# Seven block products for eight in the output phase of a hybrid decoder step

## The chip, the cores and the metric

The kernel runs on one core of one Trainium2 chip. The metric is device time in microseconds (us) of one execution. TensorE (PE) multiplies; VectorE (DVE), ScalarE (ACT) and GpSimd (POOL) work on tiles in SBUF, and DVE and ACT also on PE's accumulators in PSUM; SyncE (SP) issues the DMAs. Each engine runs its own instructions in order and waits on semaphores for the others.

## The reference

One layer of a decoder on 2048 prompt tokens and 32 sample tokens (8 sequences of 4), width 1024, everything float32:

```
h = rmsnorm(x);  p = h @ w_in                    # conv, rwkv and gate columns
y_c = bg * conv(cg * xin) * silu(zc)             # short convolution branch
y_r = (groupnorm(rwkv7_scan(...)) + bonus) * silu(zr)
m   = sigmoid(gc) * (y_c @ w_out_c) + sigmoid(gr) * (y_r @ w_out_r)
out = rmsnorm(x + m @ w_o, final_g)              # plus the new states
```

`w_out_c`, `w_out_r` and `w_o` are 1024 x 1024 each. The change concerns the last two lines of it.

## The kernel before

**Precision.** A float32 operand is kept as two float32r tiles, a rounded high part and the low rest. A product is three matmuls per 128 rows of the contraction: high weight by high data, low by high, high by low. The parts of a weight are made once (ACT copies the high part, DVE subtracts the low one), stored to DRAM (`keep`) and loaded again as 1 MB tiles `whl` for later sets. Four `whl` buffers exist; `take_w` hands out the next tile of the fixed list `order` and starts the loads of the following three.

**Sets.** The prompt is cut in four sets of 512 tokens (numbers 0 to 3 in the code, one to four in this text); the fourth carries the 32 sample tokens as well (544 columns). The first part of the program, four stretches of some 600 us, projects each set with 81 blocks of `w_in` (24 matmuls of 512 columns per block of 128 output channels, accumulator `ip`) and interleaves the scan of the rwkv branch, pair of heads by pair of heads. Its small matmuls and its DVE and ACT work are generators (`Side`) that a planner, the class `Clock`, spreads over the stretch with weights (`SIDES`) and costs of its own; on DVE and ACT the planned order is then fixed. The branch results y_c and y_r and the gates go to DRAM (`yc`, `yr`, `gc`, `gr`).

**Output phase.** Each set has three stages of 1024 x 1024: c (`w_out_c`), r (`w_out_r`) and out (`w_o`). Stages c and r give m transposed, eight blocks of 128 channels each (`proj`, tiles `ip`); DVE multiplies by 1 + tanh gate, adds c and r and splits m into `MH` and `ML` (`merged`). Stage out takes 128 tokens of m as the stationary operand and 512 columns of `w_o` as the moving one (accumulator `po`): per set two halves of four kp steps of 24 matmuls. Then x is added (`xo`), the squares are summed by ACT, and `finish` scales the row and stores it; the reciprocal root is a power on GpSimd (`rsq`). The order is: c of sets one and two at the end of the first part (`merge_first`, over the last scan), then r and out of set two, r and out of set one, then c, r and out of set three and of set four. Set four's 544 columns run as 256 and 288. `load_y` brings y and splits it for the next set while out runs. Each of the three weights is split the first time it is used, which lies in this phase.

In the profile nearly every compute row carries the line of a helper (L264), and every DMA row L337 or L264; rows are told apart by their tiles.

Of the kernel before, what the change touches and what calls it, by code (L numbers as in the profile page):

```python
# [16 lines left out]
P = 128  # L17
# [7 lines left out]
SIDES = {"first": 8.0, "late": 14.0, "keys": 30.0, "solve": 30.0, "merge": 8.0, "close": 12.0, "load": 8.0, "samp": 20.0, "out": 12.0, "prep": 10.0, "y": 4.0, "chain": 45.0, "zero": 1.0}  # L25
# [319 lines left out]
def hybrid_kernel(tc, x_prompt, x_sample, state_conv, state_shift, state_rwkv, norm_g, w_in, conv_w,  # L345
# [26 lines left out]
    wraw_p = Raws(ctx.enter_context(tc.tile_pool(name="wraw", bufs=1)), NB * P, 4, clock)  # L372
    whl_p = clock.pooled(ctx.enter_context(tc.tile_pool(name="whl", bufs=4)), "whl", 4)
    dram = ctx.enter_context(tc.tile_pool(name="dram", bufs=1, space=DRAM))
    ps_ip = clock.pooled(ctx.enter_context(tc.tile_pool(name="ps_ip", bufs=3, space=PSUM)), "ps_ip", 3)

    yc_d = [[dram.tile([P, 2, NTT[t]], F32, name=f"yc{t}_{b}") for b in range(NB // 2)] for t in range(NSETS)]
    yr_d = [[dram.tile([P, 2, NTT[t]], F32, name=f"yr{t}_{b}") for b in range(NB // 2)] for t in range(NSETS)]
    gc_d = [[dram.tile([P, NTT[t]], F32, name=f"gc{t}_{b}") for b in range(NB)] for t in range(NSETS)]
    gr_d = [[dram.tile([P, NTT[t]], F32, name=f"gr{t}_{b}") for b in range(NB)] for t in range(NSETS)]  # L380
# [9 lines left out]
    def w_advance(dma, split, load):  # L390
        while state["dma"] < min(dma, len(order)):
            _, src, _, there = order[state["dma"]]
            if not there:
                raw = wraw_p.tile()
                SP.dma_start(out=raw.rearrange("p (kt n) -> p kt n", n=src.shape[1]),
                             in_=src.rearrange("(kt p) n -> p kt n", p=P))
                raws[state["dma"]] = raw
            state["dma"] += 1
        while state["split"] < len(order):
            i = state["split"]  # L400
            _, src, keep, there = order[i]
# [3 lines left out]
            if there:  # L405
                SP.dma_start(out=hl.bitcast(F32), in_=keep)
# [4 lines left out]
            parts_[i] = tuple(hl[:, k].rearrange("p (kt n) -> p kt n", n=src.shape[1]) for k in range(2))  # L411
# [167 lines left out]
    nwt = clock.pooled(ctx.enter_context(tc.tile_pool(name="nwt", bufs=1)), "nwt", 1)  # L579
# [111 lines left out]
    r0 = 0  # L691
# [182 lines left out]
    def conv_blocks(th, b):  # L874
# [61 lines left out]
        def bg_end():  # L936
            SP.dma_start(out=yc_d[th][b // 2][:, b % 2, :], in_=o["cv"][:, 0:nt])
            o.clear()

        def gate(nm, base, dst):  # L940
# [10 lines left out]
            def end():  # L951
                SP.dma_start(out=dst[th][b], in_=g["t"][:, 0:nt])
                tmp.free(g["t"])
# [486 lines left out]
    def rwkv_out(th, p, o):  # L1440
# [40 lines left out]
        SP.dma_start(out=yr_d[th][p // 2][:, p % 2, :], in_=yo[:, 0:nt])  # L1481
# [15 lines left out]
    def merge_first(th, b):  # L1497
# [4 lines left out]
        def fetch():  # L1502
            o, t, bb = gates.pop(0)
            o["g"] = tmp.tile([P, TW], F32, name="tmp")
            SP.dma_start(out=o["g"][:, 0:NT], in_=gc_d[t][bb])
# [11 lines left out]
        def end():  # L1517
            SP.store(gc_d[th][b], o["g"][:, 0:NT], lambda g=o["g"]: tmp.free(g))
# [4 lines left out]
    def load_first(nm, th, hf):  # L1523
# [7 lines left out]
        for q in range(NB // KG):  # L1531
            raws.append(ring[len(turn) % len(ring)])
            turn.append(q)
            for i in range(KG // 2):
                SP.dma_start(out=raws[q][:, 2 * i:2 * i + 2, :],
                             in_=(yc_d if nm == "c" else yr_d)[th][q * KG // 2 + i][:, :, cs])
# [4 lines left out]

    EDGE = 3
    plan = []
# [3 lines left out]
    for th in range(NSETS):  # L1547
        for p in range(NB):
# [18 lines left out]
    def keep(key, src):  # L1567
        if key not in seen:
            seen.add(key)
            kind = (key[0],) + key[2:]  # L1570
# [3 lines left out]
            order.append((key, src, scratch[kind], there))  # L1574
# [3 lines left out]
    MERGE = [("c", 0)] + [x for b in range(NB) for x in ([("c", b + 1)] if b + 1 < NB else []) + [("r", b)]]  # L1578
    OUTW = [(half, kp) for half in range(2) for kp in range(NB // 2)]
    ORDER3 = list(PRE[::-1]) + [th for th in range(NSETS) if th not in PRE]  # L1580
    for th in ORDER3:
        for nm, b in [x for x in MERGE if x[0] == "r" or th not in PRE]:
            wsrc = w_out_c if nm == "c" else w_out_r
            keep(("o" + nm, th, b), wsrc[0][:, b * P:(b + 1) * P])
        for half, kp in OUTW:
            keep(("o", th, half, kp), w_o[0][kp * 2 * P:(kp + 1) * 2 * P, half * 512:(half + 1) * 512])

    def main_stream(parts):
        for x, c0, c1 in parts:
            kind = (x.key[0], x.key[1]) if x.key[0] in ("oc", "or") else ("prep", x.key[1])  # L1590
# [3 lines left out]
    def load_y(th, nm):  # L1594

        src = yc_d if nm == "c" else yr_d
        nt = NTT[th]
        h, l = (XH, XL) if nm == "c" else (RH, RL)

        def load(b, j):  # L1600
            raw = o2.tile([P, 1024], F32, name="yraw")[:, 0:nt]
            SP.dma_start(out=raw, in_=src[th][b][:, j, :])
            return raw
        raws = [load(0, 0)]
        for b in range(NB):
            if b + 1 < NB:
                raws.append(load((b + 1) // 2, (b + 1) % 2))
            raw = raws.pop(0)
            A.copy(h[:, b, 0:nt], raw)
            V.tensor_tensor(out=l[:, b, 0:nt], in0=raw, in1=h[:, b, 0:nt].bitcast(F32), op=ALU.subtract)  # L1610
            yield 1
# [84 lines left out]
    for th, hv, p, nx in plan:  # L1696
        total = length(hv)
# [4 lines left out]
        else:  # L1702
# [3 lines left out]
            before = (th, p)  # L1706
            if (th, p) == (0, 0):
                Side(late_setup(), "late").over(0, 0.9 * total)
        e = EDGE / 2 * NB
        if end_(th, p):  # L1710
            run_pair(th, p, total, True)
            f = [nx] + [nx + NB * NB * (i + 1) for i in range(len(PRE))]
            behind, start = job["out", LAST * NB + p - 1], nx - 6 * NB
            for (nm, t), at, back in zip([("c", t) for t in PRE] + [("r", FIRST)], f, [EDGE * NB * (NTT[th] - HN) / NT] + [e] * len(PRE)):
                for hf, x in enumerate((at - back, at)):
                    behind = job["o" + nm, t, hf] = Side(load_first(nm, t, hf), "prep", [behind], gate=x + 0.01).over(start, x)
# [5 lines left out]
    finish_sides()  # L1722
    clock.planning = False
# [12 lines left out]
    ps_o = ph3.enter_context(tc.tile_pool(name="ps_o", bufs=5, space=PSUM))  # L1736
    fg = o1.tile([P, D], F32, name="fg")
    nc.gpsimd.dma_start(out=fg, in_=final_g.partition_broadcast(P))
    WM = NT + NSAMP
    RH, RL, MH, ML = (o1.tile([P, NB, WM], F32R, name=nm) for nm in ("RH", "RL", "MH", "ML"))  # L1740

    def merged(th, b, g, gc, c0, c1, ps):

        V.scalar_tensor_tensor(out=g[:, c0:c1], in0=g[:, c0:c1], scalar=1.0, in1=ps[:, 0:c1 - c0], op0=ALU.add, op1=ALU.mult)
        V.tensor_tensor(out=g[:, c0:c1], in0=gc[:, c0:c1], in1=g[:, c0:c1], op=ALU.add)
        A.activation(out=MH[:, b, c0:c1], in_=g[:, c0:c1], func=AF.Identity, scale=0.5)
        V.scalar_tensor_tensor(out=ML[:, b, c0:c1], in0=g[:, c0:c1], scalar=0.5, in1=MH[:, b, c0:c1].bitcast(F32),
                               op0=ALU.mult, op1=ALU.subtract)

    def merge_second(b):  # L1750

        o = {}

        def fetch():
            for nm, src in (("r", gr_d), ("c", gc_d)):
                o[nm] = o2.tile([P, WM], F32, name="gt", bufs=6)
                SP.dma_start(out=o[nm][:, 0:NT], in_=src[FIRST][b])

        def begin():
# [125 lines left out]
```

## Time and profile before

| | us |
|---|---|
| median of three runs (lowest, highest) | 3168.12 (3167.94, 3169.0) |
| span of the profiled execution | 3166.9 |
| PE busy in it | 3071.6 (97%) |
| DVE busy | 1972.5 (62%) |
| ACT busy | 1256.6 (40%) |
| GpSimd busy | 316.2 (10%) |
| stretch from the end of c to the last matmul (2690 to 3154) | 464, of it PE busy 458.8 |
| from the last matmul to the end | 12.9 |

The profiled execution is 1.2 us shorter than the median of the runs. A span is counted from the first to the last instruction. Busy times of an engine are shares over the whole program, while the stages differ: in the first part DVE is busy 64 to 78% of the time, in the output phase 37%. Matmuls overlap in the pipeline, so the price of one is the distance between starts, not its duration.

### The profile page before, as it was taken

The page shows a single profiled execution, that of the slowest core. Times are in us where ns is not written, and L with a number is a line of the kernel's source. Part 1 is how long each engine was busy: PE and PEld are TensorE (multiplying, and loading weights), DVE is VectorE, ACT ScalarE, POOL GpSimd, SP SyncE. Part 2 cuts the span into 40 slices and gives each one's busy share as a digit, 9 for nine tenths or more (in the row PEclk, how much of TensorE's full clock was granted, in tenths as well). Part 3 has the DMA queues.
Part 4 walks back from the last instruction along what each step waited for, and adds up shares of the span by engine and source line. Part 5 has one row for each costly group of instructions (what it writes and reads, how often), then busy time and mean ns, then how long its engine had stood idle before and what let it go on. Part 6 is the DMA issues. An engine that isn't in the chain of part 4 may idle for free. (4 is left out here: it accounts for less than half of the span.)

```text
span 3166.9 us, 55564 instructions
## 1 busy us (share of the span) xinstructions
PE 3071.6 (97%) x21530; PEld 2630.7 (83%) x21530; DVE 1972.5 (62%) x5444; ACT 1256.6 (40%) x2583; POOL 316.2 (10%) x521
## 2 busy tenths in 40 slices
PE   7899999999999999999999999999999998999998
PEld 6678777888888888787888889998999988878896
DVE  5577777766666666666656676777677753443432
ACT  4455555544343444444444444444444431211201
POOL 2011111111111111111111110000000010000000
PEclk9899999999999999999999999999999999999999
DMA  8677777754444444444444444443444469988863
GB/s 269 234 241 234 227 226 227 239 192 162 151 164 166 166 163 162 163 163 151 161 164 164 159 152 138 149 141 131 147 148 136 165 226 313 346 324 316 315 240 120
DMA packets 252253, 621.89 MB, mean 196 GB/s; under 512 B 35210, under 2 KB 153091, under 8 KB 198230
## 3 DMA queue, kind: packets, MB, share of 16 engines
q1 hardware_dynamic: 251846, 617.82, 56.9%
q8 instruction: 170, 2.79, 0.3%
q14 instruction: 93, 0.76, 0.1%
q0 software_dynamic: 144, 0.52, 0.0%
HBM read 457.34 MB, written 160.94 MB: 195 GB/s over the span
## 5 line engine op out<-in xcount | busy, mean ns | idle before, releaser
L264 PE MATMUL ip<-XH,whl 128*128 128x512 f32 (+3 forms) x7776 | 2112.6, 352 | 34.3 <-DVE tmp L264 11.0
L264 PEld LDWEIGHTS ip<-XH,whl 128*128 128x128 f32 x7776 | 1346.6, 191 | 190.2 <-DVE whl L264 12.2
L264 PE MATMUL ip<-XL,whl 128*128 128x512 f32 (+3 forms) x3888 | 1364.7, 351 | 0.1
L264 PEld LDWEIGHTS ip<-XL,whl 128*128 128x128 f32 x3888 | 741.5, 191 | 74.5 <-issue 5.6
L264 DVE TENSOR_TENSOR tt<-Mi,X 128x60 f32<-128x60 f32 (+24 forms) x992 | 215.3, 217 | 29.9
L264 DVE TENSOR_TENSOR X<-X,tt 128x60 f32<-128x60 f32 (+24 forms) x992 | 211.7, 213 | 32.3
L264 DVE SCALAR_TENSOR_TENSOR S<-pb,pe,sp 64x64 f32<-64x64 f32 x512 | 143.6, 280 | 135.7 <-PE pb L264 128.3
L264 ACT ACTIVATE tmp<-ip,vec 128x512 f32<-128x512 f32 (+2 forms) x174 | 102.6, 592 | 281.0 <-PE ip L264 276.7
L264 ACT ACTIVATE sp<-S,pe 128x128 f32<-128x128 f32 x256 | 102.8, 402 | 265.0 <-DVE S L264 264.1
L264 ACT COPY SV<-pb 64x128 f32<-64x128 f32 x256 | 66.0, 258 | 325.0 <-PE pb L264 323.0
L264 PE MATMUL po<-whl,MH 128*128 128x512 f32 x544 | 170.4, 394 | 0.0
L264 DVE TENSOR_TENSOR UB<-pa,P 64x64 f32<-64x64 f32 x512 | 109.9, 215 | 95.8 <-PE pa L264 78.9
L264 DVE TENSOR_TENSOR whl<-wraw,whl 128x1024 fp32r<-128x1024 f32 x105 | 132.8, 1267 | 50.5 <-ACT whl L264 42.1
L264 ACT CAST whl<-wraw 128x1024 fp32r<-128x1024 f32 x105 | 108.9, 1040 | 58.9 <-PE ip L264 36.9
L264 PE MATMUL ip<-RH,whl 128*128 128x512 f32 (+2 forms) x512 | 128.4, 342 | 2.1 <-DMA whl<-w_or 1.9
L264 PEld LDWEIGHTS po<-whl,MH 128*128 128x128 f32 x544 | 102.3, 188 | 23.6
L264 ACT COPY Xbd<-Mi 32x256 f32<-32x256 f32 x128 | 88.2, 689 | 72.0 <-DVE Mi L264 69.8
L264 DVE SCALAR_TENSOR_TENSOR gt<-gt,ip 128x288 f32<-128x288 f32 (+2 forms) x67 | 36.5, 544 | 125.4 <-PE ip L264 100.8
L264 ACT ACTIVATE tmp<-ip 128x512 f32<-128x512 f32 (+2 forms) x126 | 63.0, 500 | 124.3 <-PE ip L264 124.0
L264 PEld LDWEIGHTS pb<-UB,Xbd 128*128 128x128 f32 x512 | 86.7, 189 | 30.5 <-PE ip L264 9.2
L264 PEld LDWEIGHTS pa<-S,AR 128*128 128x128 f32 x512 | 89.9, 190 | 26.5 <-DVE S L264 12.1
L264 DVE TENSOR_TENSOR GM<-pt,mask_p 128x512 f32<-128x512 f32 x128 | 82.6, 686 | 45.8 <-PE pt L264 45.6
(495 smaller groups left out, 3914.4 us busy)
## 6 DMA issues: line engine op xcount, KB each, us to landing
wraw<-in_w_in_dram SPq DMA_DIRECT2D x81, 512.0 KB
whl<-w_k SPq DMA_DIRECT2D x24, 1024.0 KB
whl<-w_r SPq DMA_DIRECT2D x24, 1024.0 KB
whl<-w_v SPq DMA_DIRECT2D x24, 1024.0 KB
whl<-w_z SPq DMA_DIRECT2D x24, 1024.0 KB
whl<-w_xin SPq DMA_DIRECT2D x24, 1024.0 KB
whl<-w_cg SPq DMA_DIRECT2D x24, 1024.0 KB
whl<-w_zc SPq DMA_DIRECT2D x24, 1024.0 KB
```

The source lines that it names most:

```text
L264: r = f(*a, **k)
```

## The change

**Arithmetic.** Two sets are taken as one product. Write a weight as 2 x 2 blocks of 512 x 512 and the data of two sets as 2 x 2 blocks too (half of the channels by set). Instead of eight block products, seven are made (Winograd's form), on sums and differences of blocks. This is done in five stages: r and out of sets one and two (pair 0), then c, r and out of sets three and four (pair 1). Stage c of sets one and two keeps its eight blocks of 128 channels per set, but stands elsewhere: set one and the first three blocks of set two at the end of the first part, the other five at the start of the output phase.

**Weights.** The sums of weight blocks (four per weight; of `w_r` block 21 alone is not needed) are made by `comb`, a new side that starts with set two and is spread over sets two and three (weight 276). It loads 128 x 512 pieces `q`, splits each piece or sum into `qs` (ACT copy, DVE subtraction) and stores it to DRAM `units`. In the output phase all weights are loaded ready from there; no weight is split in it.

**Data.** `make(n, j)` builds the operand of product n: sums of blocks (DVE, in stage out partly GpSimd), then ACT's high part and DVE's low part, into one of three rooms: `UA`, and the former `XH` and `XL`. It runs two products ahead. A merge product is 4 groups j of 12 matmuls; its accumulators stay in PSUM across products, so that shared partial sums are added by PE; `merge_out` copies (ACT) or adds, multiplies by the gate (DVE), and for stage r adds into M, on GpSimd except for the last product. `out_done` adds an output product to x. For pair 1 the 2 x 528 columns run as 264 and 264 with the same weights. The 32 sample rows of out are 32 matmuls of 64 stationary columns (`US`).

**Layout.** `yc`, `yr`, `gc` and `gr` are stored by pairs of sets; set four's stores are three DMAs instead of one (`put`).

```diff
-SIDES = {"first": 8.0, "late": 14.0, "keys": 30.0, "solve": 30.0, "merge": 8.0, "close": 12.0, "load": 8.0, "samp": 20.0, "out": 12.0, "prep": 10.0, "y": 4.0, "chain": 45.0, "zero": 1.0}
+SIDES = {"first": 8.0, "late": 14.0, "keys": 30.0, "solve": 30.0, "merge": 8.0, "close": 12.0, "load": 8.0, "samp": 20.0, "out": 12.0, "prep": 10.0, "y": 4.0, "chain": 45.0, "zero": 1.0, "comb": 276.0}
+    def put(dst, th, src):
+        c = th % 2 * HW[th // 2]
+        SP.dma_start(out=dst[:, c:c + NT], in_=src[:, 0:NT])
+        if th == LAST:
+            for i in range(2):
+                c = i * HW[1] + NT
+                SP.dma_start(out=dst[:, c:c + NSAMP // 2], in_=src[:, NT + i * (NSAMP // 2):NT + (i + 1) * (NSAMP // 2)])
+    def part_of(w, key, j, src, scale=1.0):
+        hl = qs[turns[0] % 2]
+        turns[0] += 1
+        yield 1, [src]
+        A.activation(out=hl[:, 0], in_=src, func=AF.Copy, scale=scale)
+        yield 1, [hl[:, 0]]
+        V.scalar_tensor_tensor(out=hl[:, 1], in0=src, scalar=scale, in1=hl[:, 0].bitcast(F32), op0=ALU.mult, op1=ALU.subtract)
+        SP.store(units[w][key][j // 2][:, :, j % 2 * 4 * P:(j % 2 + 1) * 4 * P], hl.bitcast(F32))
+    def combined(dst, a, b, op):
+        V.tensor_tensor(out=qr[dst], in0=qr[a], in1=qr[b], op=op)
+    def comb():
+        for w, src in (("c", w_out_c[0]), ("r", w_out_r[0]), ("o", w_o[0])):
+            for j in range(4):
...
+                    for q in ("11", "12", "21", "22") if w == "c" else ("11", "12", "22"):
+                        yield from part_of(w, q, j, qr[q])
+                    combined("22", "21", "22", add)
+                    yield from part_of(w, "s1", j, qr["22"])
...
-                for t in PRE:
-                    cm = [merge_first(t, b) for b in range(NB)]
-                    hv += by_halves(cm[:EDGE]) + whole(cm[EDGE:-EDGE]) + by_halves(cm[-EDGE:])
+                cm = [merge_first(0, b) for b in range(NB)]
+                hv += by_halves(cm[:EDGE]) + whole(cm[EDGE:-EDGE]) + by_halves(cm[-EDGE:])
+                hv += by_halves([merge_first(1, b) for b in range(EDGE)])
+    STAGES = [("r", 0), ("o", 0), ("c", 1), ("r", 1), ("o", 1)]
+    PRODUCTS = {"m": ("11", "s2", "s3", "22", "12", "s1", "s4"), "o": ("21", "11", "t2", "t3", "t4", "t1", "22")}
+            if (th, p) == (1, 0):
+                job["comb"] = Side(comb(), "comb").over(0, sum(length(x[1]) for x in plan if x[0] in (1, 2) and x[2] is not None))
-    ps_o = ph3.enter_context(tc.tile_pool(name="ps_o", bufs=5, space=PSUM))
+    acc = [ps_o.tile([P, 2, 512], F32, name=f"acc{j}") for j in range(NP)]
+    ROOMS = [o1.tile([P, 2 * NP * WQ], F32R, name="UA")] + [t.rearrange("p a b -> p (a b)")[:, 0:2 * NP * WQ] for t in (XH, XL)]
+    def make(n, j, parts=(0, 1)):
...
+        if w != "o":
+            t = at({0: "11", 2: "12", 3: "12", 4: "21", 5: "11", 6: "22"}.get(k, "11"))
+            if k == 1:
+                op(at("11"), at("12"), at("11"), sub, V)
+                t = o2.tile([P, WQ], F32, name="st")[:, 0:wd]
+                op(t, at("22"), at("11"), sub, V)
...
+        else:
+            t = at({0: "y1", 1: "x1", 3: "x1", 4: "y2", 5: "x2", 6: "y1"}.get(k, "x1"))
+            if k == 2:
+                op(at("x1"), at("x1"), at("x2"), sub, V)
+                t = Y["21"][:, j, 0:wd]
+                op(t, at("y2"), at("x1"), sub, V)
+            if k == 5:
+                op(t, t, at("y2"), add, G)
+            if k == 6:
+                op(t, t, at("y2"), sub, G)
+                op(t, t, at("x1"), add, G)
+        A.copy(room[:, 0, j, 0:wd], t)
+        V.tensor_tensor(out=room[:, 1, j, 0:wd], in0=t, in1=room[:, 0, j, 0:wd].bitcast(F32), op=sub)
+    def merge_out(w, d, k, j):
...
+        if k < 3:
+            A.copy(dst, ps)
+            return
+        g = gate_for(w, d, q, j)
+        if k == 3:
+            gate_mul(dst, ps, view(g))
+        else:
+            V.tensor_tensor(out=dst, in0=dst, in1=ps, op=ALU.add)
+            gate_mul(dst, dst, view(g))
+        if w == "r":
+            (V if q == "x2" else G).tensor_tensor(out=M[q][:, j, 0:HW[d]], in0=M[q][:, j, 0:HW[d]], in1=R[q][:, j, 0:HW[d]], op=ALU.add)
+    def merge_phase(n):
+        for j in range(NP):
+            hook(n, j)
+            if j % 2 == 0:
+                wt = take_w((w, d, PRODUCTS["m"][k], j // 2))
+            for kt in range(NP):
+                wh, wl = (x[:, j % 2 * NP + kt, :] for x in wt)
+                for i, (w_, m) in enumerate(((wh, 0), (wl, 0), (wh, 1))):
+                    for a in range(1 + d):
...
+            merge_out(w, d, k, j)
+            make(n + 2, j)
+    def out_done(d, k, j):
+        V.tensor_tensor(out=o, in0=o, in1=acc[j][:, 0, :], op=ALU.add)
+        if k in (1, 4, 5, 6):
+            square(o, r, half)
+            if k > 4:
+                finish(r, [(o_at(d, x, j), x_rows(d, x, j, y_prompt)) for x in (q[0] + "1", q[0] + "2")])
```

Three places where the order moves. The first is PE where the output phase handles its last two sets. Rows before, at the end of r of set four:

```order
L264 MATMUL ip<-RH,whl 128x288 x2
L264 MATMUL ip<-RL,whl 128x288
L264 MATMUL ip<-RH,whl 128x288 x2
L264 MATMUL ip<-RL,whl 128x288
L264 MATMUL po<-whl,MH 128x512 x2
L264 MATMUL po<-whl,ML 128x512
```

and with the change, the step from out of pair 0 to c of pair 1 (`XL`, `UA` are rooms):

```order
L264 MATMUL acc_29709<-whl,XH 128x512 x6
L264 MATMUL acc_29710<-whl,XH 128x512 x6
L264 MATMUL acc_29707<-XL,whl 128x264 x24
L264 MATMUL acc_29708<-XL,whl 128x264 x24
L264 MATMUL acc_29709<-XL,whl 128x264 x24
L264 MATMUL acc_29710<-XL,whl 128x264 x24
L264 MATMUL acc_29707<-UA,whl 128x264 x24
```

One accumulator per group j now takes 24 short matmuls in a row where 256 and 288 columns stood.

The second place is DVE from the last merge product of pair 0 (tiles `Rx2`, `acc`) to the first addition of an output product (`Ry1`); rows of the change, without counterpart before. The piece begins

```order
L264 TENSOR_TENSOR Rx2_29700<-Rx2_29700,acc0_29707 128x512
L264 SCALAR_TENSOR_TENSOR Rx2_29700<-gt_30236,Rx2_29700 128x512
L264 TENSOR_TENSOR Mx2_29696<-Mx2_29696,Rx2_29700 128x512
L264 TENSOR_TENSOR Mx1_29695<-Mx1_29695,Mx2_29696 128x512
L264 TENSOR_TENSOR Rx2_29700<-Rx2_29700,acc1_29708 128x512
L264 TENSOR_TENSOR Y21_29693<-My2_29698,Mx1_29695 128x512
```

and goes on in this way for the four groups; 24 rows after its first row it ends with the row that reads the first output accumulator:

```order
L264 TENSOR_TENSOR XH_169<-Mx1_29695,XH_169 128x512
L264 TENSOR_TENSOR Y21_29693<-My2_29698,Mx1_29695 128x512
L264 TENSOR_TENSOR XH_169<-Mx1_29695,XH_169 128x512
L264 TENSOR_TENSOR Ry1_29701<-Ry1_29701,acc0_29707 128x512
```

GpSimd's rows beside the two last merge products and this piece are 16, of which these stand in the middle:

```order
L264 TENSOR_TENSOR My2_29698<-My2_29698,Ry2_29702 128x512
L264 TENSOR_TENSOR My1_29697<-My1_29697,My2_29698 128x512
L264 TENSOR_TENSOR Mx2_29696<-Mx2_29696,My2_29698 128x512
L264 TENSOR_TENSOR My1_29697<-My1_29697,Mx1_29695 128x512
L264 TENSOR_TENSOR Mx2_29696<-Mx2_29696,My2_29698 128x512
```

Each of its four kinds of row stands there four times. Before, GpSimd had only the powers of `finish` in the output phase.

The third place is DVE within set two, in the chain that inverts a triangular block (`tt`, `X`); with the change:

```order
L264 TENSOR_TENSOR tt<-Mi,X 128x42
L264 TENSOR_TENSOR X<-X,tt 128x7x6
L264 SCALAR_TENSOR_TENSOR qs_300<-q_297,qs_300 128x512
L264 TENSOR_TENSOR q_298<-q_298,q_295 128x512
L264 TENSOR_REDUCE mu__10090<-Yc 128x8
L264 TENSOR_TENSOR tt<-Mi,X 128x35
```

Before, no `q` or `qs` row stands there; the change adds 140 such rows on DVE from the start of set two to a little before the middle of set three, and 92 `qs<-q` rows on ACT.

More of the change, by code (lines that the diff above doesn't have):

```diff
@@ L1542, in hybrid_kernel @@
     EDGE = 3
+    REST = list(range(EDGE, NB))
     plan = []
@@ L1569, in keep @@
             seen.add(key)
+            if key[0] == "oc":
+                j, a = key[2] % 4, key[2] // 4 + 1
+                cs = slice(j % 2 * 4 * P, (j % 2 + 1) * 4 * P)
+                order.append((key, None, P, [(k * 4 * P, (k + 1) * 4 * P, units["c"][f"{a}{k + 1}"][j // 2][:, :, cs]) for k in range(2)], True))
+                return
             kind = (key[0],) + key[2:]
@@ L1852, in hybrid_kernel @@
+    for j in range(NP):
+        make(1, j)
+    for n, (w, d, k) in enumerate(seq):
+        (out_phase if w == "o" else merge_phase)(n)
     SP.flush(0)
```

415 lines of the change are left out of this document (266 added, 149 removed).

## Prediction

> **What bounds the kernel now.** I read the page's busy times first, then its slices, then a table of stretches, then who waited for whom in the output phase.
>
> ```profile
> span 3166.9 us, 55564 instructions
> PE 3071.6 (97%) x21530; PEld 2630.7 (83%) x21530; DVE 1972.5 (62%) x5444; ACT 1256.6 (40%) x2583; POOL 316.2 (10%) x521
> PE   7899999999999999999999999999999998999998
> PEclk9899999999999999999999999999999999999999
> ```
>
> PE is busy in every slice, at full clock: a matmul removed is time removed, unless another engine then ends last. The stretches (us; busy time of PE, weight loads, DVE, ACT and GpSimd with instruction counts; granted clock; DMA share; GB/s) are steady set one, sets two and three, the end of the first part, a DMA peak, the output phase, the tail:
>
> ```profile
> 202.00:642.00 440.00, 434.23 (x2907) 351.17 (x2905) 341.93 (x868) 236.22 (x434) 60.15 (x83) 1.00 0.72 229
> 644.00:1246.00 602.00, 594.06 (x4048) 489.76 (x4048) 384.49 (x1123) 248.78 (x518) 69.50 (x117) 1.00 0.47 162
> 1246.00:1848.00 602.00, 593.03 (x4039) 488.41 (x4039) 384.67 (x1124) 249.82 (x520) 70.81 (x117) 1.00 0.47 161
> 2585.00:2690.00 105.00, 96.16 (x727) 91.18 (x726) 38.02 (x59) 20.37 (x24) 6.15 (x4) 0.95 0.89 309
> 2684.00:2731.00 47.00, 43.94 (x245) 38.53 (x244) 23.09 (x40) 10.93 (x16) 0.77 (x1) 0.96 0.97 361
> 2690.00:3154.00 464.00, 458.82 (x2356) 390.55 (x2354) 170.41 (x332) 81.83 (x159) 11.45 (x14) 1.00 0.76 279
> ```
>
> From 2585 to 3154 PE idles 8.8 + 5.2 = 14.0 us. The chain (start, length, what) and PE's waits name the cause, a gate load behind the stores of freshly split weights:
>
> ```profile
> 2615.20 8.74 DMA w_oc<-whl
> 2638.76 9.29 DMA tmp<-gc
> 2731.64 44.49 PE po L264 x192
> 3001.82 96.41 PE ip L264 x768
> ```
>
> ```profile
> PE ip L264 <- DVE tmp L264: 8.0, 1, 8.0
> PE ip L264 <- DVE gt L264: 3.1, 1, 3.1
> ```
>
> **1. Matmuls: -59.6 us.** Prices are distances between starts. A matmul of 512 columns: 44.49/192 = 0.2317. Of 256 columns: 42 matmuls (14 groups of three) lie between these starts, 4.94/42 = 0.1176.
>
> ```profile
> 2612.49 0.28 PE L264 MATMUL ip<-XL,whl 128*128 128x256 f32 x1
> 2617.43 0.28 PE L264 MATMUL ip<-XL,whl 128*128 128x256 f32 x1
> ```
>
> The 768 in 96.41 us are 384 of 256 and 384 of 288 columns, so 288 costs (96.41 - 45.16)/384 = 0.1335, and 264, a quarter of the way, 0.1216. By the counts of both orders the change removes 1560 of 512 columns (361.5 us), those 768 (96.4) and 288 more of 256 (33.9): 491.8. It adds 1128 of 512 and 32 sample matmuls of 512 (1160 x 0.2317 = 268.8) and 1344 of 264 (163.4): 432.2. At 0.1176 or 0.1335 for 264 the net would be -64.9 or -43.6; 264 is nearest to 256.
>
> **2. Stalls of the output phase: -10.** The first use of 24 weights reads 0.5 MB each and stores 1 MB; eight of them:
>
> ```profile
> w_oc<-whl SPq DMA_DIRECT2D x8, 1024.0 KB
> wraw<-in_w_out_c_dram SPq DMA_DIRECT2D x8, 512.0 KB
> ```
>
> All 36 MB leave this phase. What remains, from the first gate of the five c blocks to the last store, is 128 MB by the sizes of the queue's rows, over 27.8 + 2 x 77.9 + 2 x 81.7 + 85.3 = 432 us of matmuls: 296 GB/s, between the 279 at which PE lost 5.2 us and the 361 reached. Of 14 us idle, and 2 of low clock after it, I let 6 stay. Bounds: -16, and +27 if 279 were all there is (128/0.279 = 459 us).
>
> **3. The sums of weights: +2.** 140 DVE rows of 512 elements and 92 on ACT. Nearest rows:
>
> ```profile
> L264 DVE TENSOR_TENSOR RL<-yraw,RH 128x512 fp32r<-128x512 f32 x16 | 10.9, 690 | 12.3 <-ACT RH L264 12.3
> L264 ACT CAST RH<-yraw 128x512 fp32r<-128x512 f32 x16 | 9.8, 618 | 23.2 <-DMA yraw<-yr 22.2 <-PE ip L264 0.9
> ```
>
> That is 96.6 us on DVE and 56.9 on ACT, over some 860 us. PE's order there is fixed, and behind each DVE row stand rows of the inversion and the scan on which its small matmuls wait. The cover is slack, and set one shows that it is enough: with its weight splits DVE is busy 341.93/440 = 78% and PE idles 1.3%; sets two and three have 64% and 1.3 to 1.5%. The change brings them to 75%. The 61 MB added bring the DMA from 162 to some 233 GB/s; set one has 229. SP, where 140 rows more stand ahead of weight loads, mostly waits for a weight buffer:
>
> ```profile
> SPq L337 <- PE ip L264: 847.3, 145, 15.8
> ```
>
> That, with loads three blocks ahead (3 x 24 x 0.2317 = 16.7 us), also hides set four's 64 additional stores. Bounds: 0, and all 96.6.
>
> **4. The tail: -2.**
>
> ```profile
> 3153.62 0.39 PE L264 MATMUL po<-whl,ML 128*128 128x512 f32 x1
> ```
>
> ```profile
> 3160.55 1.28 DVE L264 SCALAR_TENSOR_TENSOR xo<-xo,fin,fg 128x1024 f32<-128x1024 f32 x1
> 3162.52 1.28 DVE L264 SCALAR_TENSOR_TENSOR xo<-xo,fin,fg 32x1024 f32<-32x1024 f32 x1
> ```
>
> From the last matmul's end (3154.0) the last row takes until 3163.8, and its store until 3166.9: 12.9. Afterwards DVE still has an addition, ACT's square, three rows at 2.0 (3162.52 - 3160.55) and the 3.1 of the store: about 11. Bounds: -6 (one row left) and 0.
>
> **5. DVE and GpSimd at the step from r to out: +20, and +2 of clock.** In the output phase DVE rises to some 0.69 x 72 = 50 us per stage of 78, plus eight row ends in out: covered on average. The dense place is the piece of 25 DVE rows from the last merge product. Let that product start at 0. Its first group ends at 11.1/4 = 2.8; 24 rows of 0.69 bring DVE to 19.4, and the first output addition is done at 20.1. PE finishes out's first product at 22.2, and the next product overwrites that accumulator: 2.1 us to spare. But GpSimd has 16 additions here. The trace shows what these do to DVE (start, duration):
>
> ```profile
> 644.59 0.45 DVE L264 TENSOR_TENSOR UB<-pa,P 64x64 f32<-64x64 f32 x2 [0.18 <-PE pa L264]
> 645.07 0.81 DVE L264 TENSOR_TENSOR X<-X,tt 128x31 f32<-128x31 f32 x1
> 645.91 0.19 DVE L264 TENSOR_TENSOR tt<-Mi,X 128x30 f32<-128x30 f32 x1
> ...
> 656.75 0.23 DVE L264 TENSOR_TENSOR X<-X,tt 128x64 f32<-128x64 f32 x1
> 657.01 1.21 DVE L264 TENSOR_TENSOR tt<-Mi,X 128x75 f32<-128x75 f32 x1
> ```
>
> ```profile
> 644.54 1.28 POOL L264 TENSOR_TENSOR XL<-tmp,XH 128x512 fp32r<-128x512 f32 x1 [1.72 <-ACT XH L264]
> 656.79 1.34 POOL L264 TENSOR_TENSOR XL<-tmp,XH 128x512 fp32r<-128x512 f32 x1 [3.82 <-ACT XH L264]
> ```
>
> A DVE row of 0.19 lasts 0.81 until GpSimd ends at 645.82, one of 0.23 lasts 1.21 until 658.13; `UB<-pa,P`, whose one input is in PSUM, runs beside. GpSimd got in between DVE rows that follow each other. The Trainium skill, SBUF — State Buffer, section "Who interferes with whom", says it as a rule: a DVE instruction with two SBUF inputs and a GpSimd one that reads SBUF exclude each other for a whole instruction. By that rule the sum is the one taken here, without it the first rival's; these rows agree with it.
>
> So in the last merge product 8 additions of 1.31 (10.5 us) go into DVE's order, less the four PSUM rows beside (2.8) and the spare 2.1: 5.6 late. The product before brings 12 DVE rows (8.3), 8 additions (10.5), less 2.8: 16.0 against its 11.1, so DVE comes 4.9 late. Sum 10.5 for pair 0; pair 1, with products of 11.7 but 528 elements, about 9.5. PE stops in pieces of some 4 us, since each accumulator is waited for. After stalls the granted clock falls (0.95 in 2585 to 2690); I add 1 us each. Bounds: 0, and 15 each if DVE never runs beside a GpSimd addition. Elsewhere the additions meet a DVE with 3 us or more per product to spare.
>
> **Sum.** 3166.9 - 59.6 - 10 + 2 - 2 + 20 + 2 = 3119.3; the median of the runs lies 1.2 above the profiled execution: **3120.5 us**.
>
> **Rivals.**
> - *No exclusion at the step* (DVE keeps ahead, or GpSimd is done early): term 5 is 0, 3098.5 us. For: DVE has 2.1 us to spare without it, and GpSimd rows such as those above are few so far. Against: both rows above.
> - *DVE ends last at more steps*: in the last two out products fall 8 output additions (5.5 us), 8 row ends (some 2.1 each, 16.8) and 16 sums and splits (11.0), 33 us against 22; operands built two products ahead hide most of it. 9 us more: 3130.
> - *The DMA bounds the phase*: 27 us instead of the gain of 10, while the stops of term 5 (22) hide in it: 3120.5 + 37 - 22 = 3135. For: the share is 0.76 to 0.97. Against: 361 GB/s reached.
> - *Slower*: the sums in sets two and three reach PE, because each of the 140 rows delays a matmul of the fixed order by its 0.69: 94.6 more than taken, 3215. It decides from 57% of that on (3168.1 - 3120.5 = 47.6, and 6.3 for a slower that shows, 54 of 94.6). For: the place of the rows, in the midst of inversions. Against: set one.
>
> **How the numbers follow.** Forecast 0.55, alone 3106 to 3132; no exclusion 0.25, 3090 to 3106; more steps 0.08; DMA 0.07; slower 0.05. The range is 3091 to 3133: it leaves out the slower case, most of the DMA's and the edges. About 0.2% (6 us) is what a measurement can tell from no change. Only the slower case ends above 3174.5, in four fifths of its weight; a mild form of it lies near no change. Faster 0.94, same 0.02, slower 0.04.
>
> **What would show it.** In the profile of the changed kernel: 264-column matmuls at 0.1216 from start to start (term 1); no DMA wait over 2 us on PE from the five c blocks on (2); PE idle within 10 us of 8 per set in sets two and three (3); 11 us after the last matmul (4); PE waits of 3 to 5 us on DVE where `po`-like products begin, twice 10 in all, with two-SBUF-input DVE rows of more than 1.2 us beside GpSimd's additions (5). It would be wrong if those waits are missing, if PE waits for `whl` loads in the new phase, or if sets two and three grow by more than 10 us together.

## The result, and the profile after

The changed kernel takes **3117.33 us** (median of 4 runs, 3114.32 to 3118.26) against 3168.32 (4 runs, 3167.94 to 3169.0): ratio 0.9833, 95% interval 0.9819 to 0.9847. The forecast was 3120.5 us in a range of 3091 to 3133. The profiled execution has a span of 3115.7 us, 51.2 less than the 3166.9 before. The page of the changed kernel, its span, busy times and some slices:

```profile
span 3115.7 us, 56464 instructions
PE 3017.7 (97%) x21418; PEld 2583.1 (83%) x21418; DVE 2157.3 (69%) x5713; ACT 1339.5 (43%) x2744; POOL 389.5 (13%) x568
...
PE   7899999999999999999999999999999999999998
...
POOL 2011111111111110111111111000000000030040
```

GpSimd's slices before the change:

```profile
POOL 2011111111111111111111110000000010000000
```

PE's share is the same 97%: what left is its own work. GpSimd has two new peaks, at the two steps from r to out. Who kept PE waiting from the end of the first part on (total, times, longest, us):

```profile
PE acc L264 <- DVE Rx L264: 10.2, 4, 3.2
PE acc L264 <- DVE Ry L264: 2.1, 1, 2.1
PE acc L264 <- ACT XH L264: 1.7, 1, 1.7
PE acc L264 <- DMA whl<-uo: 1.0, 1, 1.0
PE acc L264 <- DVE My L264: 0.9, 1, 0.9
```

The 8.0 and 3.1 us behind `tmp` and `gt` are gone; no transfer holds PE for more than 1.0. In their place stand waits on DVE. The timeline of PE at the first step (start, length, in brackets the wait before it) shows them where out's first products begin:

```profile
2755.67 2.94 PE L264 MATMUL acc<-whl,XH 128*128 128x512 f32 x12
...
2760.75 1.88 PE L264 MATMUL acc<-whl,XH 128*128 128x512 f32 x6 [2.14 <-DVE Rx L264]
...
2765.54 8.71 PE L264 MATMUL acc<-whl,XH 128*128 128x512 f32 x30 [2.91 <-DVE Rx L264]
...
2775.99 4.18 PE L264 MATMUL acc<-whl,XL 128*128 128x512 f32 x17 [1.74 <-ACT XH L264]
```

The stretches of the end of the first part with the c blocks, of this step, of c of pair 1, and of the second step, that of pair 1 (columns as in the prediction):

```profile
2595.00:2679.30 84.30, 82.92 (x542) 74.42 (x536) 27.04 (x51) 11.90 (x18) 4.52 (x3) 1.00 0.93 320
2757.00:2776.00 19.00, 12.21 (x44) 8.73 (x43) 18.93 (x20) 4.56 (x8) 10.78 (x7) 0.82 0.57 208
2853.00:2934.00 81.00, 81.00 (x665) 81.00 (x664) 53.95 (x93) 23.24 (x38) 0.96 (x1) 1.00 0.89 317
2990.00:3035.00 45.00, 37.76 (x222) 32.30 (x221) 39.41 (x44) 8.04 (x15) 24.97 (x16) 0.96 0.58 203
```

The stretch that idled 8.8 of 105 us before runs almost without a stop at 320 GB/s. At the step PE idles 6.8 of 19 us, and the clock granted is 0.82. DVE is busy in all of it (18.93). At the second step PE idles 7.2 of 45 us at 0.96.

A measure that helps with all that follows: the group of 36 small matmuls near the end of the first part stands in every kernel. From its start to the end of the last matmul (here called the **output stretch**) and from there to the span's end (the **tail**) there is nothing but what the change touches.

```profile
2594.15 1.27 PE L264 MATMUL pt<-SV,GM 128*64 128x64 f32 x36
...
3094.90 8.73 PE L264 MATMUL acc<-whl,XH 128*128 128x512 f32 x37
...
3111.58 0.74 DVE L264 SCALAR_TENSOR_TENSOR Rx<-Rx,fin,fg 128x512 f32<-128x512 f32 x1
```

The same group in the kernel before:

```profile
2588.66 1.27 PE L264 MATMUL pt<-SV,GM 128*64 128x64 f32 x36
```

After: output stretch 3103.63 - 2594.15 = 509.5, tail 3115.7 - 3103.63 = 12.1. Before (last matmul's end 3154.01): 565.4 and 12.9. So of the 51.2 us, 55.9 were gained in the output stretch and 0.8 in the tail, and 5.5 were lost in the first part.

### The profile page after: what moved, and what is told of

The parts are those of the page before. It is cut to its first block, busy times and chain, and to the rows that moved or that the text cites. A ratio compares the mean times of both kernels' runs of the same rounds, so it can differ in the third digit from the quotient of the medians.

```text
span 3115.7 us, 56464 instructions
## 1 busy us (share of the span) xinstructions
PE 3017.7 (97%) x21418; PEld 2583.1 (83%) x21418; DVE 2157.3 (69%) x5713; ACT 1339.5 (43%) x2744; POOL 389.5 (13%) x568
## 5 line engine op out<-in xcount | busy, mean ns | idle before, releaser
L264 PE MATMUL ip<-XH,whl 128*128 128x512 f32 (+3 forms) x7088 | 1944.9, 354 | 22.9 <-DVE whl L264 10.5
L264 PEld LDWEIGHTS ip<-XH,whl 128*128 128x128 f32 x7088 | 1225.9, 190 | 168.4 <-DVE whl L264 13.2
L264 PE MATMUL ip<-XL,whl 128*128 128x512 f32 (+3 forms) x3544 | 1250.4, 353 | 0.8 <-POOL XL L264 0.8
L264 PEld LDWEIGHTS ip<-XL,whl 128*128 128x128 f32 x3544 | 672.9, 190 | 71.5 <-issue 5.6
L264 DVE TENSOR_TENSOR whl<-wraw,whl 128x1024 fp32r<-128x1024 f32 x81 | 102.3, 1264 | 24.8 <-ACT whl L264 24.0
L264 PEld LDWEIGHTS pa<-S,AR 128*128 128x128 f32 x512 | 88.9, 189 | 27.3 <-DVE S L264 14.9
L264 POOL COPY carry<-tmp 128x1 f32<-128x1 f32 x99 | 22.3, 225 | 708.2 <-ACT tmp L264 708.2
L264 PE MATMUL pb<-UB,Xbd 128*128 128x128 f32 x512 | 104.3, 285 | 3.9 <-DVE UB L264 3.1
L264 PEld LDWEIGHTS pb<-SV,BKt 128*128 128x128 f32 x512 | 89.8, 189 | 20.4 <-ACT SV L264 6.1
L264 PE MATMUL pa<-S,AR 128*128 128x128 f32 x512 | 102.1, 281 | 4.7 <-DVE S L264 4.5
L264 PE MATMUL pb<-SV,BKt 128*128 128x128 f32 x512 | 100.7, 278 | 1.4 <-ACT SV L264 1.4
```

Source lines behind the costliest of these rows:

```text
L264: r = f(*a, **k)
```

## The experiments

Times are medians; each is compared with the kernel before on the same chip (3167.1 to 3169.0 throughout). The theory was that of the prediction: matmuls removed pay in full, and at the steps GpSimd's additions hold DVE back and DVE holds PE. Its rivals: DVE simply has too many rows there, or PE waits for results of GpSimd.

**1. The sums of out's operands on DVE.**

```diff
-                op(t, t, at("y2"), add, G)
+                op(t, t, at("y2"), add, V)
```

and the same for the two sums of the last operand.

> The changed kernel with the 24 sums of out's last two operands on DVE instead of GpSimd, so that GpSimd keeps only the additions into M of stage r. Exclusion (GpSimd additions hold back two-SBUF-input DVE rows): of the 16 GpSimd additions at each step from r to out 4 to 5 remain; the DVE rows of 1.7 us go, PE stops at most 2 us per step instead of 7, and the time is 3102 to 3107 us against 3117.3. Plain load (DVE simply has too many rows at the step): DVE has 24 rows of 0.69 more, 16.6 us, 4 to 5 of each 12 of them at the step; the stops stay or grow, 3117 to 3122 us.

3105.53 us (3102.2 to 3107.93), ratio 0.9803 (0.9786 to 0.9819). DVE has 24 rows more and the kernel is 12 us faster. PE's waits on DVE and ACT from the first product of r on are down from 14.9 to 2.9 us:

```profile
PE acc L264 <- DVE Rx L264: 2.9, 3, 1.4
PE acc L264 <- DMA whl<-uo: 0.9, 1, 0.9
```

Output stretch 493.2, 16.3 less. That speaks against plain load.

**2. All additions on DVE**, those of experiment 1 and the ones into M:

```diff
-            (V if q == "x2" else G).tensor_tensor(out=M[q]...
+            V.tensor_tensor(out=M[q]...
```

> As the run before, and also the additions into M on DVE: GpSimd adds nothing any more in the output phase. Exclusion: the product before the last of r has 20 DVE rows of 0.69, 13.8 us against 11.1 of PE, the last has 24; after the 2.1 us that DVE has to spare 0.6 us per step remain; 3101 to 3106 us, no DVE row of 128x512 over 0.8 us in the output phase. Plain load: 48 rows more on DVE, 33 us, more stops than in the changed kernel, 3120 to 3130 us.

3104.25 us (3102.32 to 3107.55), ratio 0.9799 (0.9784 to 0.9813). With 48 more DVE rows PE waits for nothing at the steps, and the output stretch is 490.4. DVE's rows of one kind in the output phase, grouped by form (total, mean ns), first of the changed kernel:

```profile
L264 DVE TENSOR_TENSOR Rx<-Rx,acc 128x512 f32<-128x512 f32 x30 | 20.5, 684 | 14.3 <-PE acc L264 14.2
...
L264 DVE TENSOR_TENSOR Y<-My,Mx 128x512 f32<-128x512 f32 x8 | 11.9, 1493 | 0.0
...
L264 DVE TENSOR_TENSOR XL<-Mx,XL 128x512 fp32r<-128x512 f32 x8 | 11.7, 1506 | 0.0
```

and of this experiment:

```profile
L264 DVE TENSOR_TENSOR XL<-Mx,XL 128x512 fp32r<-128x512 f32 x8 | 5.5, 683 | 0.0
...
L264 DVE TENSOR_TENSOR Y<-My,Mx 128x512 f32<-128x512 f32 x8 | 5.4, 683 | 0.0
```

The same row took 1493 ns on average beside GpSimd and takes 683 without. Rows with one input in PSUM (`Rx<-Rx,acc`, `Ry<-Ry,acc`) were never stretched: in the changed kernel none of 512 elements lasts over 0.69 us, and two of them (2739.19 and 2741.97, 0.69 us each) lie wholly within an addition of GpSimd.

**3. The sums of weights without their ACT and DVE rows.** `part_of` stores a constant tile; `combined` does nothing.

> The changed kernel without the ACT and DVE rows of the sums of weights (92 and 140); the pieces are loaded and all the stores made, but from a constant tile, so the weights of the output phase are constants. Theory: the 5 us by which sets two and three grew come from these rows, in PE's waits and in the order of PE's rows around them; the time falls by 4 to 6 us to 3111 to 3113, set two by 4. Rival: they come from the 61 MB of transfers or not from comb at all: 3116 to 3118, set two stays 4 us longer than before the change.

3111.26 us (3110.99 to 3115.43), ratio 0.9823 (0.9808 to 0.9838): within the expected time, 6 us below the changed kernel. Where the 6 us lie depends on the marks. Between ACT's `lora` rows, with which each set begins, sets two and three last 607.8 and 604.7, nearly as with the sums (608.5 and 604.8). But that row stands elsewhere among PE's matmuls here: 13 more of these fall into set two. So the stretch is better taken between two groups of PE's own matmuls (`pt<-SV,GM`), one 96 us before set two begins and one 151 us before set three ends in the kernel before. It holds all rows of the sums, and PE has the same matmuls in it in every kernel (columns as in the prediction). Before, changed, this experiment, and experiment 6, which comes below:

```profile
581.81:1735.07 1153.26, 1135.73 (x7791) 935.98 (x7790) 746.84 (x2155) 488.06 (x1006) 139.63 (x227) 1.00 0.49 167
582.20:1740.11 1157.91, 1141.14 (x7792) 934.79 (x7791) 829.34 (x2295) 539.50 (x1098) 143.41 (x227) 1.00 0.64 218
579.28:1734.07 1154.79, 1135.30 (x7792) 934.05 (x7791) 748.50 (x2155) 490.86 (x1006) 141.77 (x227) 1.00 0.57 194
582.87:1736.58 1153.71, 1139.25 (x7791) 932.78 (x7790) 888.90 (x2387) 594.93 (x1190) 144.59 (x227) 1.00 0.64 219
```

Of the 4.6 us that the change adds here, 3.1 are gone without the rows, half of this run's gain; the other half lies ahead, where no edit is. PE's idle time did not grow with the sums (17.5 before, 16.8 with them); its busy time did, by 5.4 us for the same matmuls. These stand in another order: between neighbouring groups of this kind there are up to 23 more or fewer of them than before, in this experiment at most 12, and almost only near one place. So the rows and the order that the planner makes for them went together, and no run separates the two. One profile has its limits as well: the eight with these rows lie between 1155.6 and 1160.6, that of experiment 4, without them, at 1150.5.

**4. The kernel before with its output weights ready** and, not shown, a copy of 1 MB per pair of heads in sets two to four that fills them with other values.

```diff
+                if key[0] in ("oc", "or", "o"):
+                    there = True
+                    ready.append(scratch[kind])
```

> The kernel before, with one thing of the change alone: the 24 output weights are never split, they are loaded ready (1 MB each) also at their first use. They hold other values (columns of w_in, copied from DRAM to DRAM in sets two to four, 1 MB per pair of heads). Theory: the first uses, 0.5 MB read, split and 1 MB stored, caused the stalls before r and their low clock: the time falls by 16 to 19 us to 3149 to 3152, no DMA wait over 2 us on PE after 2590. Rival, as the sum had it: part of the stalls stays, since gates and y keep the queues as full; 8 to 10 us less, 3158 to 3160. Other rival: the stalls went with the new order of the output phase, not with the splits: 3165 to 3168.

3156.56 us (3155.29 to 3157.87), ratio 0.9963 (0.995 to 0.9976): 12 us faster by this alone, between the first two expectations. Its one long wait after the first part:

```profile
PE ip L264 <- DVE gt L264: 5.1, 1, 5.1
```

Output stretch 553.4, 12.0 less. The first uses of the weights (reading, splitting and storing together) made three quarters of the stalls; one gate stall stays in the old order of the phase.

**5. Additions that nothing reads.** On the first experiment's kernel:

```diff
+            if k > 4:
+                for i in range(k - 4):
+                    G.tensor_tensor(out=idle[i], in0=idle[i], in1=M[q][:, j, 0:NT], op=ALU.add)
```

> The first experiment's kernel (sums of out's operands on DVE, 3105.5 us) with 12 additions of 128x512 more on GpSimd at each step from r to out, into two tiles that nothing reads. Exclusion: it does not matter whose additions they are; DVE rows of 1.2 to 1.8 us come back, PE stops 5 to 8 us per step again, 3115 to 3120 us. Late data (PE waited for results of GpSimd, not for DVE held back): nothing waits for these additions, 3103 to 3108 us.

3119.05 us (3118.5 to 3122.81), ratio 0.9846 (0.9828 to 0.9863): the 12 us are gone again, though PE needs none of these results. Output stretch 513.6; PE stops 9.3 and 9.0 us at the two steps, a little more than expected. Rows of DVE and GpSimd at the first step, from the timeline:

```profile
2758.74 0.68 DVE L264 TENSOR_TENSOR Rx<-Rx,acc 128x512 f32<-128x512 f32 x1
2758.97 2.95 POOL L264 TENSOR_TENSOR idle<-idle,Mx 128x512 f32<-128x512 f32 x2 [1.90 <-DVE Mx L264]
2759.34 1.44 DVE L264 TENSOR_TENSOR Mx<-Mx,Mx 128x512 f32<-128x512 f32 x1
2760.71 1.76 DVE L264 SCALAR_TENSOR_TENSOR Rx<-gt,Rx 128x512 f32<-128x512 f32 x1
2762.39 0.68 DVE L264 TENSOR_TENSOR Y<-My,Mx 128x512 f32<-128x512 f32 x1
```

Two additions back to back turn two DVE rows of 0.68 into 1.44 and 1.76; the row after them is short again. This excludes the rival of late data: DVE waits for results of GpSimd 7.5 us at the two steps, no more than in experiment 1 (7.6), and in the changed kernel it never waits there for one. With experiments 1 and 2 it shows the exclusion. It is the rule that the prediction took from the Trainium skill, SBUF — State Buffer, section "Who interferes with whom"; its other half, that a row with at most one SBUF input is free of it (outside DVE's modes that use both ports), agrees too (0.68 and 0.69 for rows such as `Rx<-Rx,acc`).

**6. The splits of weights twice.**

```diff
-        A.activation(out=hl[:, 0], in_=src, func=AF.Copy, scale=scale)
+        for i in range(2):
+            A.activation(out=hl[:, 0], in_=src, func=AF.Copy, scale=scale)
```

and DVE's subtraction likewise.

> The changed kernel with every ACT copy and every DVE subtraction of the pieces of output weights done twice in sets two and three (92 DVE rows and 92 ACT rows more, some 63 and 57 us). Cover: PE has slack for them, DVE comes to some 84% in these sets; 3117 to 3122 us. Each row delays PE by its length (the slower rival): 3117 + 63 = 3180 us. Between them: if the first dose cost 5 us, this one costs 5 to 10.

3115.57 us (3113.92 to 3122.91), ratio 0.9835 (0.9817 to 0.9854): no difference from the changed kernel. In set two DVE is busy 482 of 608 us (it was 389 before the change):

```profile
678.00:1286.00 608.00, 600.42 (x4064) 490.23 (x4065) 482.14 (x1283) 323.99 (x648) 76.13 (x118) 1.00 0.67 229
```

The slower rival, where each row delays PE by its length, is out. As a second dose it is not clean: the planner gave PE yet another order (up to 43 matmuls more or fewer between two groups), and the stretch of experiment 3 lasts 1153.7, with 14.5 us idle.

**7. A shorter row end**, on the second experiment's kernel.

```diff
+            if half == 0 and m == P:
+                A.activation(out=t, in_=t, func=AF.Identity, scale=f)
+            else:
+                V.scalar_tensor_tensor(...)
+            if k < 5:
+                V.tensor_tensor(out=o, in0=o, in1=fg[:, 0:4 * P], op=ALU.mult)
```

> The second experiment's kernel (no additions on GpSimd in the output phase, 3104.3 us), and a shorter row end: the half of each row that is complete early is multiplied by final_g when it is complete, so that at the end ACT only scales it and DVE has one row of 0.75 per row end instead of two. Theory: the tail is DVE's rows behind the last matmul; 0.7 of addition, 0.8 of ACT's square, 0.15 x 6 and GpSimd's 0.55, one row of 0.75, 3.4 to the end of the store: 7 to 8 us after the last matmul instead of 12.1, 3099 to 3101 us. Rival: ACT's row or the store ends last, 11 to 12 us, 3103 to 3105.

3093.87 us (3091.68 to 3095.85), ratio 0.9762 (0.9747 to 0.9777): less than expected, and not for the reason expected. The tail is 10.3 us, not 7 to 8. The last matmuls and DVE's last row end:

```profile
3073.68 8.71 PE L264 MATMUL acc<-whl,XH 128*128 128x512 f32 x37
...
3084.45 0.16 DVE L264 TENSOR_TENSOR nw<-fin 128x1 f32<-128x1 f32 x1 [0.44 <-POOL fin L264]
3084.53 0.68 DVE L264 TENSOR_TENSOR Rx<-Rx,acc 128x512 f32<-128x512 f32 x1
...
3087.44 0.16 DVE L264 TENSOR_TENSOR nw<-fin 128x1 f32<-128x1 f32 x1 [0.73 <-POOL fin L264]
...
3088.21 0.75 DVE L264 SCALAR_TENSOR_TENSOR Rx<-Rx,fin,fg 128x512 f32<-128x512 f32 x1
```

The row ends still follow each other: PE is done at 3082.4, but DVE waits in its order for the power of an earlier row on GpSimd before it takes the last addition at 3084.5. The tail accounts for 1.9 us of the 10 gained on experiment 2; experiments 10 and 11 ask for the rest.

**8. The changed kernel again.**

> The changed kernel once more, for the spread between executions of its first part, in which its edits and those of the first two experiments are alike. If sets two and three were 4.6 us longer than before because of the sums, they are so again within 1 us (608.5 and 604.8); if the spread is as large as the effect, either set lies 2 us or more beside these.

3115.95 us (3112.01 to 3120.26). Sets two and three: 608.5 and 604.7, as in the first profile of this kernel within 0.1. That is closer than the spread: over the eight profiles with the same rows the two sets together last 1211.1 to 1216.0, before the change 1208.6. Output stretch 509.5, again. But set one, whose rows are the same in every kernel here, lasts 641.5 instead of 636.7. The passage from set two to set three in the kernel before (from 75 us ahead of ACT's `lora` row to 10 us behind it):

```profile
1206.93:1291.93 85.00, 79.97 (x626) 71.21 (x626) 58.52 (x158) 35.06 (x74) 10.92 (x15) 0.98 0.45 158
```

in the changed kernel:

```profile
1211.51:1296.51 85.00, 77.86 (x606) 69.98 (x605) 67.61 (x167) 36.81 (x79) 10.61 (x15) 0.94 0.63 211
```

in experiment 3, without the rows:

```profile
1205.54:1290.54 85.00, 79.15 (x622) 70.53 (x621) 58.59 (x156) 34.91 (x74) 10.86 (x15) 0.98 0.44 154
```

There the operands of the next set are prepared and DVE is needed at once. With the sums (67.6 us of DVE instead of 58.5) PE idles 2.1 us more, and at a clock of 0.94 instead of 0.98 loses at most another 3 (85 x 0.04, an estimate). Experiment 8 shows 76.89 at 0.96, experiment 6 78.00 at 0.98.

**9. The sums early**, on the seventh experiment's kernel, and, not shown, ACT scales the first half of the sample rows too.

```diff
-.over(0, sum(length(x[1]) for x in plan if x[0] in (1, 2) and x[2] is not None))
+.over(0, 0.85 * sum(length(x[1]) for x in plan if x[0] == 1 and x[2] is not None))
```

> The seventh experiment's kernel (3093.9 us) with two things changed: the sums of weights are spread over the first 85% of set two, at 2.4 times the pace, instead of sets two and three, so that none is left at the passage from set two to set three, where PE idled 2 to 3 us more in every profile with the sums; and the first half of the sample rows is scaled by ACT too (one DVE row of 0.7 less in the tail). Theory: the cost of the sums lies where the next set's operands are prepared and DVE was busy 57 of 70 us instead of 52; PE is busy there 80 of 85 us again instead of 76.6 to 77.9, sets two and three together are 2 to 5 us shorter, the tail 0.7; 3088 to 3092 us. Rival: at 2.4 times the pace DVE's or the queues' slack in the midst of set two is used up (DVE 426 of 525 us, some 280 GB/s), and set two grows by more than the passage gains: 3095 to 3105.

3089.93 us (3085.68 to 3094.05), ratio 0.975 (0.9736 to 0.9765). In this run six of the 92 pieces of weights, by the order of rows and stores in the program, took the values of a later piece (the 18 of experiment 12's text is three times that). Sets two and three are 605.8 and 604.8, the tail 9.9. At the passage PE is busy 79.66 of 85 us, as before the change; but the stretch of experiment 3 lasts 1155.2, still 1.9 more than there.

**10 and 11. The seventh and the second kernel again**, beside the ninth.

> The seventh experiment's kernel once more, beside the ninth. If its 10 us under the second experiment's kernel are its own, 3092 to 3096 us again, though only 1.8 of them lie in the tail; if they came from the spread of the first part, 3098 to 3105.

> The second experiment's kernel once more, beside the seventh. Its profile had a first part 8 to 12 us longer than the others at the same edits. If that is the spread between executions or chips, 3095 to 3100 us, 2 to 4 above the seventh's; if it is the kernel's own, 3102 to 3107 again.

3096.38 (3094.74 to 3099.72), ratio 0.9772 (0.9757 to 0.9786), and 3101.3 (3097.05 to 3107.56), ratio 0.9784 (0.9766 to 0.9802). The seventh is ahead again, by 5 instead of 10 us; both times lie between the two that were expected, so they don't decide. Output stretches 488.6 and 490.3, tails 10.2 and 12.1: 3.6 us of the 7.7 between the two profiled executions (3095.6 and 3103.3). The rest lies in the first part, whose PE rows are the same in both. The second kernel's four executions show how far that goes: 3097.1 and 3097.6 us with a granted clock of 0.995 over the whole, 3105.0 and 3107.6 with 0.991.

**12. The sums early, each store issued before its buffer is written again.**

```diff
+        if any(x[1].tensor.name == hl.tensor.name for x in SP.due):
+            SP.flush(0)
```

> The ninth experiment's kernel (3089.9 us), in which 18 of the 92 pieces of weights were stored only after their buffer had taken the next piece; here a store that is still due is issued before its buffer is written again. Nothing else differs. Theory: the order of 18 stores on the queue costs nothing, 3087 to 3093 us, sets two and three 1210 to 1212 us together, the tail 9.9. Rival: SP now waits for the splitting row ahead of each such store and weight loads behind it come late, PE waits for whl in set two, over 3095.

3100.24 us (3091.97 to 3101.98, 5 runs), ratio 0.9775 (0.976 to 0.9791), outside the theory's range. PE doesn't wait for `whl` in set two, so the rival's reason doesn't hold either. Set one lasted 641.1 in this profile, set two 608.2. Moving the sums shows no gain that can be told from the spread of the first part. The best kernel tried is the seventh: 0.9762 and 0.9772 against 0.9833 for the change.

## Why the prediction was right

The sum came out 3.6 us too high (3119.3 against a span of 3115.7). That it came so close is in part luck: single terms were off by up to 6.5 us, in both directions.

1. **Matmuls, -59.6: held.** In c of pair 1 the products of 96 matmuls with 264 columns start 11.75 us apart (2854.57, 2866.32): 0.1224 each, against 0.1216. Over 1344 of them that is 1 us.

```profile
2854.57 11.91 PE L264 MATMUL acc<-UA,whl 128*128 128x264 f32 x96
2866.32 11.91 PE L264 MATMUL acc<-XH,whl 128*128 128x264 f32 x96
```

2. **Stalls, -10: right cause, too small.** With GpSimd's additions gone (experiment 2) the output stretch is 490.4, 75.0 less than before; less the 58.5 of the matmuls this leaves 16.5. So about all of the 14 us of idle time and the 2 of clock went, not all but 6. The step that failed is the estimate that 6 us would stay because 296 GB/s lies between the 279 at which PE lost time and the 361 reached: the stretch at 320 ran almost without a stop. Not the rate stalled PE, but the first uses of the weights, with single loads behind their stores (12 of the 16 us, experiment 4), and one gate in the old order.

3. **Sums of weights, +2: mis-sized, about 5.** Sets two and three grew by 4.6 us, by 2.5 to 7.4 over the eight profiles with these rows. DVE has room for them, as experiment 6 shows with more of them. What the step missed is that PE's idle time is not where they cost: over the two sets it stayed the same (17.0 before, 16.5 after). So the test named there, idle time within 10 us of 8 per set, passed (9.9 in set two) and could not have shown it. The growth is busy time of PE, for the same matmuls in another order (experiment 3). The prediction called that order fixed; it is fixed within a kernel, but the planner made another one for the kernel with the sums. The passage to the next set, where 9 us more of DVE in 85 cost PE 2 to 3 us of idle time, is a part of it at most: experiment 9 mended the passage, and its stretch is still 1.9 us longer than before. What of the rows, the order and the granted clock makes the 5 us stays open.

4. **Tail, -2: -0.8.** The sum left out that the row ends queue: each needs some 2.2 us of DVE in order, waits for powers on GpSimd included, and four stand at the end, as long as PE's last 37 matmuls (8.7 us).

5. **The step from r to out, +20 and +2: held, and it decided.** The output stretch with the exclusion less the one without, 509.5 - 490.4, is 19.1. The picture was different in its pieces: PE stopped six times for 1.7 to 3.2 us, 14 us in all, not twice 10, and the remaining 5 go for the most part with the lower clock. The clock can account for at most (1 - 0.82) x 19 = 3.4 at the first step and (1 - 0.96) x 45 = 1.8 at the second, and less where it was low while PE stood still. Counted from starts, the first 48 matmuls of out need 11.1 us at 0.2317 and took 20.3 (2755.67 to 2775.99) with 6.8 of stops, which leaves 2.4; the second step leaves 2.3 in the same way, somewhat more than its clock accounts for. So the idle time was taken too high and what goes beside it too low. GpSimd didn't hold DVE for each addition: it waited for DVE's results as well, and between two additions one DVE row got in.

With the measured terms: 3166.9 - 58.5 - 16.5 + 5.5 - 0.8 + 19.1 = 3115.7. The rivals: "no exclusion" is out, and its 3098.5 is about what experiments 1, 2 and 11 gave (3101 to 3106) once the additions were moved. More steps with DVE last, DMA as the bound and the slower case did not occur: from the end of the first part on, PE's other waits are 0.5 and 0.9 us on DVE and 1.0 on a transfer.

## What to carry to other kernels

Count the rows that one engine must do between the last result of a stage and the first need of the next, not its share of the stage; and before work is given to an idle engine, ask whether its reads exclude the engine it is to relieve: here 48 additions put on GpSimd to spare DVE cost 19 us, and back on DVE nothing that shows. To judge a change in one phase of a long program, measure that phase between two rows that stand in all variants, on the engine that bounds it: it repeats to 2 us here, where the whole time spreads over ten, and marks on another engine shift with the order.

## What was not expected of the hardware

The first part differs between executions although its rows don't. Set one, from ACT's first `lora` row to that of set two, in experiment 5 and in experiment 8:

```profile
41.73:675.34 633.61, 608.89 (x3955) 491.37 (x3954) 468.02 (x1177) 325.06 (x593) 77.52 (x115) 0.99 0.74 238
39.36:680.89 641.53, 616.81 (x3954) 496.73 (x3953) 468.19 (x1178) 325.02 (x592) 77.39 (x115) 0.98 0.73 236
```

PE idles 24.7 us in both. All 7.9 us of difference are busy time of PE, 1.2% more for the same matmuls, at a granted clock lower by about as much. The same 17 us near the start of set one, again in experiment 5 and in experiment 8:

```profile
95.00:112.00 17.00, 14.80 (x80) 11.13 (x80) 10.95 (x14) 9.38 (x17) 1.45 (x5) 1.00 0.90 330
95.00:112.00 17.00, 15.98 (x51) 11.75 (x52) 7.51 (x10) 5.42 (x11) 1.20 (x4) 0.51 0.78 267
```

PE was granted the full clock there in the one and half of it in the other (1.00 and 0.51). So between these two it is the granted clock that differs, and in experiment 11 the whole time goes with it; why it is granted differently was not found. The output stretch repeats to 0.1 us in two profiles of the changed kernel (509.5), to 0.2 in two of experiment 2's, and to 1.9 in two of experiment 7's.

The granted clock also fell (0.82 over 19 us) after stops of only 1.7 to 2.9 us each. What the stops brought beside their own 14 us is some 5 us at the two steps, most of it the clock.
